# One branch instead of two in the last expert pair, whole combination ahead of its up projection, and an output norm that passes through PSUM

## The chip, the cores and the metric

The kernel runs on one core of one Trainium2 chip. The metric is the device time of one execution in microseconds (us), median of the runs shown. All times of the trace are counted from the start of the profiled execution's span.

## The reference

Two layers over 512 tokens of width 1024 (float32). Each layer is a mixer and a mixture of experts, each with a residual and a layer norm behind it. Layer 0's mixer has two convolutions, layer 1's a spatial gating unit and chunked attention.

```
for layer in range(2):
    mix = conv_shortconv_mixer(x, ...) if layer % 2 == 0 else sgu_chunk_attention_mixer(x, ...)
    x = layer_norm(ALPHA * x + mix, mix_ln_g[layer], mix_ln_b[layer])
    ffn = hierarchical_moe(x, ...)      # 4 groups x 8 experts, the two best of one group
    x = layer_norm(ALPHA * x + ffn, ffn_ln_g[layer], ffn_ln_b[layer])
...
hb = silu(xb @ w_gate[e]) * (xb @ w_up[e]);   y = hb @ w_down[e]
```

An expert's gate and up matrices are 1024 x 512, its down matrix 512 x 1024. All 32 experts of a layer are run, whatever the routing.

## The kernel before, in words

**The experts.** `experts()` runs the 32 experts of a layer as 16 pairs, g = 0 to 15. A pair has 128 slots, 64 for each expert. Tokens that do not fit into them are treated in conditional code. For each pair TensorE (PE) does, in this order:

- the gate projection into PSUM tile `pg` (32 matmuls, L746); ScalarE (ACT) turns it into `sg` (L756)
- the up projection into `pu` (32 matmuls, L746); VectorE (DVE) multiplies `sg` and `pu` to the hidden tile `h` (L761)
- four transposes of `h` (L767), which ACT copies to `hT` (L769)
- a branch, `If v > 0` (L1156), on a count `v` that the routing left in `nxi`: behind it lies `overflow(v)`, code for slots that are full. It is skipped here in nearly all pairs
- the down projection in two halves, `py` (16 matmuls each, L746). ACT and DVE split each half into a high and a low part `y` (L779, L780).

**The combination.** `combine(S, *prev, ts)` adds the output of the pair before to the accumulator `acc`: for each of 4 token tiles and 2 halves a pair of matmuls with the one-hot matrix `S` (L790, L791) and one DVE addition (L799). In the last pair two of the four tiles are combined ahead of the up projection and two behind it (L1127, L1141).

**The general loop.** `crowded()` (L1035) holds a general loop over all pairs for inputs with very many tokens on an expert. It stands ahead of the last pair's gate, in an `If most > 0` (L1037). Here it is skipped in both layers, so each engine jumps over its body. `most` is counted, and PE gets a hint of the branch, at the end of pair 14. PE alone gets hints, in the other branches too. Behind it `last()` loads the first weights of the next mixer (L1609).

**The end of a layer.** The last pair's output is combined half by half by `Last.half` (L801 ff.): PE puts `acc` of tiles 0 and 1 into PSUM (L815), adds the spread of `y`, and DVE takes the statistics (L826). Tiles 2 and 3 are added on DVE (L825). `hat()` (L284) normalises tiles 0 and 1 on ACT, out of PSUM into `acc`, tile by tile. Layer 0 goes on in `mixer1` with `turn(0)`, transposes of `acc` (L1341), then matmuls against high and low parts of the weights (L1377 ff.). Layer 1 goes on in `output()`, which scales by `gf` and adds `bf`: GpSimd (POOL) on 3.5 of the 4 halves of tiles 0 and 1 (L1592, L1593), DVE on the rest. Of tiles 2 and 3, DVE does the norm itself, two operations per half (L1602, L1603). Each finished half is written to the output.

**Order of the work.** Each engine executes its own instructions in the order of the program. A branch is executed by every engine. The weights come over the queue of SyncE (SP), in the order of `ws.load`.

Of the kernel before, what the change touches and what calls it, by code (L numbers as in the profile page):

```python
# [31 lines left out]
PQ = 256  # L32
# [11 lines left out]
def trunk(ctx: ExitStack, tc: tile.TileContext, a, out, layers=2, moe=True):  # L44
# [236 lines left out]
    def hat(t, mr, ys):  # L281
        n = D // len(ys)
        for h, y in enumerate(ys):
            ACT.activation(acc[:, t, h * n:(h + 1) * n], y, AF.Identity, bias=mr[2], scale=mr[1])  # L284
# [157 lines left out]
    class Router:  # L442
# [178 lines left out]
        def counts(self):  # L621
# [8 lines left out]
            nxs = small([2 * NP + 1], "nxs")  # L630
# [13 lines left out]
            DVE.tensor_reduce(nxs[:, 2 * NP:], m, axis=AX.X, op=OP.max)  # L644
            nxi = small([2 * NP + 1], "nxi", I32)
# [118 lines left out]
    def hidden_T(h):  # L764
        p = mtile((128, 4, 128))
        for j in range(4):
            PE.transpose(p[:, j], h[:, j * 128:(j + 1) * 128], ident)  # L767
        hT = wk.tile([128, 4, 128], F32, name="hT", tag="q2")
        ACT.activation(hT, p, AF.Copy)  # L769
        return hT  # L770
# [30 lines left out]
    class Last:  # L801
# [6 lines left out]
        def half(self, h, S, yh, yl):  # L808
# [9 lines left out]
            for t in range(NT):  # L818
                if t == 2 and h:
                    self.mrs = self.finish(0)  # L820
                    self.lead(1)
                    for i in range(2):
                        hat(i, self.mrs[i], self.ys[i])
# [146 lines left out]
    def count(nxi, i, **kw):  # L970
        return nc.values_load(nxi[0:1, i:i + 1], min_val=0, max_val=NTHR + 1,
# [6 lines left out]
    def experts(rt, ws, T1, pt, x1d, xt, xg, xg2, update, last, last2, lead, finish):  # L978
# [56 lines left out]
        def crowded():  # L1035
            slots = ws.order[6:8]
            with tc.If(most > 0, label=f"most{ws.l}", preferred_fallthrough_block=True):  # L1037
                for g in range(NP):
                    v, cond = when(nxi, NP + g, 0)
                    with cond:  # L1040
# [4 lines left out]
                        with tc.For_i(0, v, 1):  # L1045
# [9 lines left out]
                            h3 = hidden_T(hidden(h3, proj2("u", xo, *u)))  # L1055
                            u = [ws.fetch(0, 4 + j, slots[j], g) for j in range(2)]
                            y3 = down(h3, *u, T3.wt[:, 0:1], (yh, yl))
                            combine(onehot_S(T3.tk[:, 0:1], "q2"), *y3)

        for g in range(NP):  # L1060
            W = lambda j: ws.u[6 * g + j]
            own, own2 = EVEN if COLS[g] < HEAVY else ODD
            if g == NP - 1:
                crowded()
                last()
# [58 lines left out]
            if g:  # L1124
                S = onehot_S(col(T1.tk, g - 1))
                if g == NP - 1:
                    combine(S, *prev, (0, 1))  # L1127
# [5 lines left out]
            if g > 1:  # L1133
                v = count(nxi, COLS[g])
# [5 lines left out]
            else:  # L1140
                combine(S, *prev, range(2 if g == NP - 1 else 0, CM if g < NP - 1 else NT))  # L1141
# [13 lines left out]
            if g > 1:  # L1155
                with tc.If(v > 0, label=skip, preferred_fallthrough_block=True):  # L1156
                    overflow(v)
# [5 lines left out]
            if g == NP - 2:  # L1163
                most = count(nxi, 2 * NP)
                tc.mark_branch_hint_location(f"most{ws.l}", most > 0, engines=[ET.PE])
# [162 lines left out]
    def mixer1(prev, ws):  # L1328
# [32 lines left out]
        ys, mrs = combine_last(prev, lambda: turn(0))  # L1361
# [221 lines left out]
    def output(prev):  # L1583
# [11 lines left out]
        for t, s in ((0, slice(0, 512)), (0, slice(512, 1024)), (1, slice(0, 512)), (1, slice(512, 512 + PQ))):  # L1595
            scale_shift(POOL, t, s)
        scale_shift(DVE, 1, slice(512 + PQ, 1024))
        for t in (2, 3):
            for h in range(2):
                s = slice(512 * h, 512 * h + 512)  # L1600
                x = acc[:, t, s]
# [108 lines left out]
```

## Time and profile before

| | us |
|---|---|
| median of 3 runs (1438.19 to 1445.37) | 1443.88 |
| profiled execution, its own time | 1442.83 |
| its span | 1440.9 |
| PE busy | 1333.4 (93%) |
| DVE busy | 684.5 (48%) |
| ACT busy | 370.3 (26%) |
| POOL busy | 294.7 (20%) |
| mean granted clock of PE | 0.976 |

The profiled execution is 1.05 us under the median. A share of busy time is a mean over stages. The last pair of either layer and the stretch behind it are short, and there the waits count: what one engine was waiting for, and when that came.

### The profile page before, as it was taken

How to read it: one execution, taken by the hardware profiler on the slowest of the kernel's cores; microseconds unless marked ns; L12 is line 12 of the kernel's file. 1: busy time of each engine (PE TensorE's matmuls, PEld its weight loads, DVE VectorE, ACT ScalarE, POOL GpSimd, SP SyncE). 2: the span in 40 equal slices, each digit the busy share in tenths (PEclk: the TensorE clock that was granted, in tenths of full speed). 3: DMA queues.
4: the chain of work that ended last, by engine and by line, in shares of the span. 5: the costliest groups of instructions: out<-in, count | busy, mean ns of one | idle time of the engine just before them, and what ended most of it. 6: DMA issues, size and time to landing. Idle time of an engine off the chain costs nothing. (4 is left out here: it accounts for less than half of the span.)

```text
span 1440.9 us, 19633 instructions
## 1 busy us (share of the span) xinstructions
PE 1333.4 (93%) x7322; PEld 705.9 (49%) x7322; DVE 684.5 (48%) x1412; ACT 370.3 (26%) x701; POOL 294.7 (20%) x262
## 2 busy tenths in 40 slices
PE   9989999998999998898899999999999999989984
PEld 6777764333353334333586767834333444333331
DVE  7997688323342223322628554794322343322326
ACT  5545541111111111111525555511111111111101
POOL 5784620000000000000653239200000000000002
PEclk9999999999999999999999999999999999999997
DMA  7505469999999999999500037689999999999971
GB/s 294 234 5 212 175 243 428 419 424 422 419 403 412 422 419 426 422 418 354 206 1 1 23 133 315 257 338 421 420 425 424 421 394 420 427 422 422 423 301 59
DMA packets 56837, 461.21 MB, mean 320 GB/s; under 512 B 8804, under 2 KB 9444, under 8 KB 33232
## 3 DMA queue, kind: packets, MB, share of 16 engines
q1 hardware_dynamic: 51184, 449.96, 75.8%
q0 software_dynamic: 4608, 7.79, 1.5%
q8 instruction: 102, 1.67, 0.5%
q10 hardware_dynamic: 864, 1.13, 0.2%
q14 instruction: 79, 0.65, 0.1%
HBM read 461.56 MB, written 6.29 MB: 325 GB/s over the span
## 5 line engine op out<-in xcount | busy, mean ns | idle before, releaser
L746 PE MATMUL py<-w,hT 128*64 128x512 f32 (+1 forms) x1280 | 243.2, 617 | 22.3 <-issue 11.6
L746 PE MATMUL pu<-w,xt 128*64 128x512 f32 (+1 forms) x1280 | 244.2, 607 | 19.8 <-DMA w<-in_w_up_dram 19.8
L746 PE MATMUL pg<-w,xt 128*64 128x512 f32 (+1 forms) x1280 | 233.4, 599 | 10.9 <-ACTq L1037 10.9
L761 DVE TENSOR_TENSOR h<-sg,pu 128x512 f32<-128x512 f32 x32 | 22.0, 688 | 355.9 <-issue 302.1
L691 POOL DMA_INDIRECT xg<-x1d,idx x30 | 29.7, 990 | 780.2 <-PE m L439 677.9
L746 PEld LDWEIGHTS pu<-w,xt 128*64 128x64 f32 (+1 forms) x1280 | 78.3, 129 | 176.3 <-issue 143.2
L799 DVE TENSOR_TENSOR acc<-acc,m 128x512 f32<-128x512 f32 x240 | 148.6, 680 | 19.3 <-PE m L791 17.3
L746 PEld LDWEIGHTS pg<-w,xt 128*64 128x64 f32 (+1 forms) x1280 | 76.2, 128 | 163.1 <-issue 140.8
L746 PEld LDWEIGHTS py<-w,hT 128*64 128x64 f32 (+1 forms) x1280 | 72.4, 128 | 154.5 <-issue 150.4
L780 DVE SCALAR_TENSOR_TENSOR y<-py,wt,y 128x512 fp32r<-128x512 f32 x64 | 48.0, 750 | 199.2 <-ACT y L779 199.2
L779 ACT ACTIVATE y<-py,wt 128x512 fp32r<-128x512 f32 x64 | 44.0, 687 | 302.9 <-PE py L746 302.9
L790 PE MATMUL m<-y,S 128*128 128x512 f32 x248 | 106.1, 428 | 0.0
L791 PE MATMUL m<-y,S 128*128 128x512 f32 x248 | 98.0, 395 | 0.0
L109 POOL TENSOR_TENSOR wl<-win,wh 128x512 fp32r<-128x512 f32 x64 | 84.2, 1331 | 65.6 <-ACT wh L108 65.4
L769 ACT ACTIVATE hT<-m 128x512 f32<-128x512 f32 x32 | 19.1, 597 | 292.4 <-PE m L767 270.5
L109 POOL TENSOR_TENSOR wl<-wo,wh 128x512 fp32r<-128x512 f32 x64 | 82.1, 1309 | 38.2 <-ACT wh L108 37.8
L756 ACT ACTIVATE sg<-pg 128x512 f32<-128x512 f32 x32 | 19.1, 597 | 217.3 <-PE pg L746 217.3
L790 PEld LDWEIGHTS m<-y,S 128*128 128x128 f32 x248 | 46.8, 189 | 39.3 <-issue 26.9
L128 PE MATMUL m<-xh,wl 128*128 128x512 f32 x144 | 57.6, 400 | 3.0 <-POOL wl L109 3.0
L127 PE MATMUL m<-xh,wh 128*128 128x512 f32 x144 | 57.4, 399 | 0.8 <-ACT wh L108 0.8
L129 PE MATMUL m<-xl,wh 128*128 128x512 f32 x144 | 56.8, 394 | 0.0
L791 PEld LDWEIGHTS m<-y,S 128*128 128x128 f32 x248 | 46.9, 189 | 7.9 <-DVE y L780 1.0
(446 smaller groups left out, 1881.2 us busy)
## 6 DMA issues: line engine op xcount, KB each, us to landing
w<-in_w_gate_dram SPq DMA_DIRECT2D x64, 2048.0 KB, 24.9
w<-in_w_up_dram SPq DMA_DIRECT2D x50, 2048.0 KB, 18.2
w<-in_w_down_dram SPq DMA_DIRECT2D x50, 2048.0 KB, 21.0
w<-in_w_up_dram SPq DMA_DIRECT2D x40, 512.0 KB, 25.0
w<-in_w_down_dram SPq DMA_DIRECT2D x40, 512.0 KB, 22.8
win<-in_w_in_dram SPq DMA_DIRECT2D x18, 512.0 KB, 7.8
wo<-in_w_out_dram SPq DMA_DIRECT2D x4, 2048.0 KB, 12.3
w<-in_w_up_dram SPq DMA_DIRECT2D x8, 1024.0 KB, 15.8
```

The source lines that it names most:

```text
L109: POOL.tensor_tensor(l, src, h, op=OP.subtract)
L127: PE.matmul(p, wh[:, j], xh[:, k], start=(k == 0), stop=False)
L128: PE.matmul(p, wl[:, j], xh[:, k], start=False, stop=False)
L129: PE.matmul(p, wh[:, j], xl[:, k], start=False, stop=(k == KD - 1))
L691: POOL.indirect_dma_start(out=dst, out_offset=None, in_=x1d, in_offset=bass.IndirectOffsetOnAxis(ap=idx_col, axis=0), bounds_check=T - 1, ...
L746: PE.matmul(p[w * c:w * c + w], x[:, w * c:w * c + w], ww[own[w * c // SUB]], **kw)
L761: DVE.tensor_mul(h, sg, pu)
L779: ACT.activation(yh[:, s], p, AF.Copy, scale=wt)
L780: DVE.scalar_tensor_tensor(yl[:, s], p, wt, yh[:, s], op0=OP.mult, op1=OP.subtract)
L790: PE.matmul(p, S[:, t * 128:(t + 1) * 128], yh[:, s], start=start, stop=False)
L791: PE.matmul(p, S[:, t * 128:(t + 1) * 128], yl[:, s], start=False, stop=True)
L799: DVE.tensor_add(acc[:, t, s], acc[:, t, s], p)
```

## The change

It has five parts.

1. **One branch.** The counts `nxi` get one more entry, the sum of `most` and the last pair's count. The branch on `most` ahead of the last pair is gone. The last pair's branch (L1156) asks for the sum. Inside it stand a branch to the pair's overflow code and, behind that, the branch to the general loop. `last()` follows behind. The hint to PE stands ahead of the up projection, as in other pairs.
2. **Combination.** In the last pair all four tiles are combined ahead of the up projection, none between it and the transposes.
3. **Norm of tiles 0 and 1** half by half: tile 0 and 1 first halves, then tile 0 and 1 second halves.
4. **Ten filler matmuls** (`keep_warm(10)`, bf16, 128 x 512) ahead of `turn(0)`.
5. **Output norm.** ACT writes the normed halves of tiles 2 and 3 into PSUM (`pg`, `pu`, `py`, `py`); DVE multiplies there by `gf`, and adds `bf` into `acc`. POOL does all four halves of tiles 0 and 1.

```
-            DVE.tensor_reduce(nxs[:, 2 * NP:], m, axis=AX.X, op=OP.max)
-            nxi = small([2 * NP + 1], "nxi", I32)
+            DVE.tensor_reduce(nxs[:, 2 * NP:2 * NP + 1], m, axis=AX.X, op=OP.max)
+            TT(nxs[:, 2 * NP + 1:], nxs[:, 2 * NP:2 * NP + 1], n[:, COLS[-1]:COLS[-1] + 1], op=OP.add)
+            nxi = small([2 * NP + 2], "nxi", I32)
...
-                    for i in range(2):
-                        hat(i, self.mrs[i], self.ys[i])
+                    for j in range(2):
+                        for i in range(2):
+                            hat(i, self.mrs[i], self.ys[i], j)
...
-            with tc.If(most > 0, label=f"most{ws.l}", preferred_fallthrough_block=True):
+            with when(nxi, 2 * NP, 0)[1]:
...
-            if g == NP - 1:
-                crowded()
-                last()
...
-                    combine(S, *prev, (0, 1))
+                    combine(S, *prev)
...
-                v = count(nxi, COLS[g])
+                v = count(nxi, COLS[g] if g < NP - 1 else 2 * NP + 1)
...
-                combine(S, *prev, range(2 if g == NP - 1 else 0, CM if g < NP - 1 else NT))
+                combine(S, *prev, range(0, CM if g < NP - 1 else 0))
...
                 with tc.If(v > 0, label=skip, preferred_fallthrough_block=True):
-                    overflow(v)
+                    if g < NP - 1:
+                        overflow(v)
+                    else:
+                        v1, cond = when(nxi, COLS[g], 0)
+                        with cond:
+                            overflow(v1)
+                        crowded()
+                if g == NP - 1:
+                    last()
...
-            if g == NP - 2:
-                most = count(nxi, 2 * NP)
-                tc.mark_branch_hint_location(f"most{ws.l}", most > 0, engines=[ET.PE])
...
-        ys, mrs = combine_last(prev, lambda: turn(0))
+        def first_turn():
+            keep_warm(10)
+            turn(0)
+        ys, mrs = combine_last(prev, first_turn)
...
-        for t, s in ((0, slice(0, 512)), (0, slice(512, 1024)), (1, slice(0, 512)), (1, slice(512, 512 + PQ))):
-            scale_shift(POOL, t, s)
-        scale_shift(DVE, 1, slice(512 + PQ, 1024))
+        norms = {}
+        for t in (2, 3):
+            for h in range(2):
+                p = norms[t, h] = ptile("gu"[h] if t == 2 else f"y{h}")
+                ACT.activation(p, ys[t][h], AF.Identity, bias=mrs[t][2], scale=mrs[t][1])
+        for t in (0, 1):
+            for h in range(2):
+                scale_shift(POOL, t, slice(512 * h, 512 * h + 512))
...
-                x = acc[:, t, s]
-                DVE.scalar_tensor_tensor(x, ys[t][h], mrs[t][0], gf[:, s], op0=OP.subtract, op1=OP.mult)
-                DVE.scalar_tensor_tensor(x, x, mrs[t][1], bf[:, s], op0=OP.mult, op1=OP.add)
+                p = norms[t, h]
+                TT(p, p, gf[:, s], op=OP.mult)
+                TT(acc[:, t, s], p, bf[:, s], op=OP.add)
```

The order of the instructions on ACT, around the end of layer 0's pair 14 and the last pair. Line numbers of the changed kernel are a few higher: L779 is L781 there, L756 is L758, L769 is L771. In the kernel before:

```order
L779 ACTIVATE y<-py_10645,wt_1956 128x512
L703 ACTIVATE xt<-m,gb 128x128 x4
L779 ACTIVATE y<-py_10675,wt_1956 128x512
L1037 COMPARE_AND_BRANCH
...
L1037 UNCONDITIONAL_BRANCH
L756 ACTIVATE sg<-pg 128x512
L971 TENSOR_LOAD nxi
L769 ACTIVATE hT<-m 128x512
L1156 COMPARE_AND_BRANCH
```

In the changed kernel:

```order
L781 ACTIVATE y<-py_10666,wt_1957 128x512
L758 ACTIVATE sg<-pg 128x512
L974 TENSOR_LOAD nxi
L771 ACTIVATE hT<-m 128x512
L1156 COMPARE_AND_BRANCH
L974 TENSOR_LOAD nxi
L1161 COMPARE_AND_BRANCH
...
L1156 UNCONDITIONAL_BRANCH
L806 ACT_TABLE_LOAD
L806 ACTIVATE warm<-mean_w 128x1
L781 ACTIVATE y<-py_14301,wt_1957 128x512
```

The long body (225 listed rows of ACT between branch and target in the kernel before, 252 in the changed one) has moved from ahead of `sg` to behind `hT`, and the jump over the short body is gone.

PE at the same place, in the kernel before:

```order
L746 MATMUL py_10675<-w,hT 64x512 x8
L1037 COMPARE_AND_BRANCH
...
L1037 UNCONDITIONAL_BRANCH
L746 MATMUL pg<-w,xt 64x512 x16
L790 MATMUL m<-y,S 128x512
L791 MATMUL m<-y,S 128x512
...
L746 MATMUL pu<-w,xt 64x512 x16
...
L767 MATMUL m<-ident,h 128x128 x4
L1156 COMPARE_AND_BRANCH
```

In the changed kernel:

```order
L748 MATMUL py_10666<-w,hT 64x512 x8
L748 MATMUL pg<-w,xt 64x512 x16
L792 MATMUL m<-y,S 128x512
L793 MATMUL m<-y,S 128x512
...
L1135 REGISTER_ALU
L1719 BRANCH_PREFETCH_HINT
L748 MATMUL pu<-w,xt 64x512 x16
L769 MATMUL m<-ident,h 128x128 x4
L1156 COMPARE_AND_BRANCH
```

The 16 combining matmuls (L792, L793) now stand together between the gate and up projections, nothing stands between the up projection and the transposes, and one branch is left.

DVE at the end of the program, in the kernel before:

```order
L275 SCALAR_TENSOR_TENSOR mvr<-mv_29012,mvr 128x2
L1592 TENSOR_TENSOR acc<-acc,gf 128x256
L1593 TENSOR_TENSOR acc<-acc,bf 128x256
L1602 SCALAR_TENSOR_TENSOR acc<-acc,mv_29012,gf 128x512
L1603 SCALAR_TENSOR_TENSOR acc<-acc,mvr,bf 128x512
```

In the changed kernel:

```order
L274 SCALAR_TENSOR_TENSOR mvr<-mv_29035,mvr 128x2
L1615 TENSOR_TENSOR pg<-pg,gf 128x512
L1616 TENSOR_TENSOR acc<-pg,bf 128x512
L1615 TENSOR_TENSOR pu<-pu,gf 128x512
L1616 TENSOR_TENSOR acc<-pu,bf 128x512
```

The two operations on 128 x 256 are gone from DVE. Four pairs of operations remain, now with one operand in PSUM each (two of the four are shown on the changed side, one on the other).

## Rows read from the trace of the kernel before

**Rows 1.** What PE waited for, whole program: us in total, times, longest.

```profile
PE pg L746 <- ACTq L1037: 10.9, 2, 5.5
```

**Rows 2.** Timeline of PE, last pair of layer 0: start, us, instruction, idle before.

```profile
655.17 8.46 PE L746 MATMUL pg<-w,xt 128*64 128x512 f32 x32 [5.45 <-ACTq L1037]
...
674.60 0.60 PE L767 MATMUL m<-ident,h 128*128 128x128 f32 x4
675.94 3.65 PE L746 MATMUL py<-w,hT 128*64 128x512 f32 x16 [0.74 <-ACTq L1156]
```

**Rows 3.** Timeline of PE, last pair of layer 1.

```profile
1384.82 8.86 PE L746 MATMUL pg<-w,xt 128*64 128x512 f32 x32 [5.44 <-ACTq L1037]
...
1405.98 3.65 PE L746 MATMUL py<-w,hT 128*64 128x512 f32 x16 [0.74 <-ACTq L1156]
```

**Rows 4.** Windows: us, busy (x) PE, PEld, DVE, ACT, POOL; PEclk, DMA share, GB/s.

```profile
655.17:663.56 8.39, 8.39 (x33) 2.55 (x33) 0.48 (x1) 0.00 (x0) 0.00 (x0) 0.83 0.87 314
665.62:672.64 7.02, 7.02 (x33) 2.21 (x33) 1.19 (x2) 0.00 (x0) 0.00 (x0) 1.00 1.01 430
...
1384.82:1393.61 8.79, 8.79 (x33) 2.62 (x33) 0.49 (x1) 0.00 (x0) 0.00 (x0) 0.79 0.91 338
1395.66:1402.67 7.01, 7.01 (x33) 2.21 (x32) 1.19 (x2) 0.00 (x0) 0.00 (x0) 1.00 0.44 167
```

**Rows 5.** Line 1037 (the long jump), 640 to 700 us: ns, first and last start.

```profile
L1037 ACTq EVENT_SEMAPHORE  x2: 17/17/17, 655.1 to 655.2; - x2
...
L1037 ACTq COMPARE_BRANCH  x1: 45/45/45, 649.8 to 649.8; - x1
```

**Rows 6.** Line 1037, whole program, PE's own sequencer, one jump in each layer.

```profile
L1037 PEldq COMPARE_BRANCH  x2: 2867/4458/6049, 646.1 to 1375.7; - x2
```

**Rows 7.** Line 1156 (the short jump), 640 to 700 us.

```profile
L1156 ACTq COMPARE_BRANCH  x1: 45/45/45, 675.3 to 675.3; - x1
L1156 ACTq EVENT_SEMAPHORE  x1: 17/17/17, 675.9 to 675.9; - x1
```

**Rows 8.** Timeline of DVE, last pair of layer 0, the hidden tile.

```profile
672.83 0.69 DVE L761 TENSOR_TENSOR h<-sg,pu 128x512 f32<-128x512 f32 x1 [6.02 <-PE pu L746]
```

**Rows 9.** Timeline of ACT, last pair of layer 0, the copy `hT`.

```profile
675.29 0.60 ACT L769 ACTIVATE hT<-m 128x512 f32<-128x512 f32 x1 [10.96 <-PEq L1156]
```

**Rows 10.** DMA queues of the page: packets, MB, share of 16 engines.

```profile
q14 instruction: 79, 0.65, 0.1%
```

**Rows 11.** Timeline of ACT behind layer 0, the four normed halves.

```profile
693.15 2.79 ACT L284 ACTIVATE acc<-m,mvr 128x512 f32<-128x512 f32 x4 [0.87 <-DVE mvr L275]
```

**Rows 12.** Timeline of PE behind layer 0, the transposes.

```profile
693.98 0.33 PE L1341 MATMUL m<-ident,acc 128*128 128x128 f32 x1 [3.25 <-ACT acc L284]
695.32 3.31 PE L1341 MATMUL m<-ident,acc 128*128 128x128 f32 x15 [1.01 <-ACT acc L284]
```

**Rows 13.** Timeline of PE, filler matmuls at the start and later.

```profile
0.93 4.45 PE L148 MATMUL m<-onesb 128*128 128x512 bf16 x10 [0.93 <-DVE onesb L163]
...
198.17 1.25 PE L148 MATMUL m<-onesb 128*128 128x512 bf16 x5
```

**Rows 14.** Timeline of DVE at the program's end.

```profile
1423.51 0.67 DVE L825 TENSOR_TENSOR acc<-acc,py 128x512 f32<-128x512 f32 x1
...
1427.43 0.91 DVE L275 SCALAR_TENSOR_TENSOR mvr<-mv,mvr 128x2 f32<-128x2 f32 x1
...
1430.00 1.75 DVE L1602 SCALAR_TENSOR_TENSOR acc<-acc,mv,gf 128x512 f32<-128x512 f32 x1
...
1436.94 0.75 DVE L1603 SCALAR_TENSOR_TENSOR acc<-acc,mvr,bf 128x512 f32<-128x512 f32 x1
```

**Rows 15.** Timeline of POOL at the program's end, its first operation.

```profile
1423.16 1.26 POOL L1592 TENSOR_TENSOR acc<-acc,gf 128x512 f32<-128x512 f32 x1 [78.99 <-ACT acc L284]
```

**Rows 16.** Groups by shape: ACT from SBUF into PSUM.

```profile
L312 ACT ACTIVATE py<-apad,par 128x512 f32<-128x512 f32 x2 | 1.6, 782 | 7.2 <-DVE apad L398 7.2
```

**Rows 17.** DMA issues of the page or its view: KB each, us to landing.

```profile
out_dram<-acc SPq DMA_DIRECT2D x4, 256.0 KB, 2.0
```

More of the change, by code (lines that the diff above doesn't have):

```diff
@@ L31 @@
 CM = 1
-PQ = 256
 W0 = 10
@@ L279, in two, with hat @@
         return [y[:, 0:512], y[:, 512:1024]]
-    def hat(t, mr, ys):
+    def hat(t, mr, ys, only=None):
         n = D // len(ys)
         for h, y in enumerate(ys):
+            if only not in (None, h):
+                continue
             ACT.activation(acc[:, t, h * n:(h + 1) * n], y, AF.Identity, bias=mr[2], scale=mr[1])
@@ L629, in counts @@
                 TT(over[:, i], cs, lim[:, i], op=OP.is_gt)
-            nxs = small([2 * NP + 1], "nxs")
+            nxs = small([2 * NP + 2], "nxs")
             n, m = nxs[:, 0:NP], nxs[:, NP:2 * NP]
@@ L762, in hidden, with hidden_T @@
         return h
-    def hidden_T(h):
+    def hidden_T(h, tag="q2"):
         p = mtile((128, 4, 128))
@@ L767, in hidden_T @@
             PE.transpose(p[:, j], h[:, j * 128:(j + 1) * 128], ident)
-        hT = wk.tile([128, 4, 128], F32, name="hT", tag="q2")
+        hT = wk.tile([128, 4, 128], F32, name="hT", tag=tag)
         ACT.activation(hT, p, AF.Copy)
@@ L970, in count @@
     def count(nxi, i, **kw):
-        return nc.values_load(nxi[0:1, i:i + 1], min_val=0, max_val=NTHR + 1,
+        return nc.values_load(nxi[0:1, i:i + 1], min_val=0, max_val=NTHR + 1 + WIDE,
                               skip_runtime_bounds_check_because="a count of blocks", **kw)
@@ L1054, in crowded @@
                             u = [ws.fetch(0, 2 + j, slots[j], g) for j in range(2)]
-                            h3 = hidden_T(hidden(h3, proj2("u", xo, *u)))
+                            h3 = hidden_T(hidden(h3, proj2("u", xo, *u)), "q3")
                             u = [ws.fetch(0, 4 + j, slots[j], g) for j in range(2)]
                             y3 = down(h3, *u, T3.wt[:, 0:1], (yh, yl))
-                            combine(onehot_S(T3.tk[:, 0:1], "q2"), *y3)
+                            combine(onehot_S(T3.tk[:, 0:1], "r"), *y3)
         for g in range(NP):
```

## The prediction

> **What bounds the kernel now.** I read the page first (PE is busy for 93% of the span), then the list of what PE waited for, then the timelines around the largest wait that the diff touches. That wait is the long jump: PE stands twice for some 5.5 us ahead of the last pair's gate, for ACT's sequencer at line 1037 [rows 1]. The timelines show it in both layers [rows 2, 3]: the end of pair 14's down projection lies at 655.17 - 5.45 = 649.72 and at 1384.82 - 5.44 = 1379.38 us. The wait for ACT is a jump, not work: ACT took its branch at 649.8 and sent its event at 655.1, so the long jump takes 5.3 us [rows 5]. The short jump over a pair's overflow code takes 675.9 - 675.3 = 0.6 us [rows 7]. In the last pair itself PE waits for no weights, so it is paced by PE's own work and by these jumps. Behind the long wait PE's granted clock is low: the gate takes 8.39 us at 0.83, where the same 32 matmuls of up take 7.02 at 1.00; in layer 1 it is 8.79 at 0.79 against 7.01 [rows 4]. [...] At the program's end DVE and POOL share the output norm and DVE ends last: its last operation ends at 1437.69, and its half lands 2.0 us later [rows 14, 17].
>
> **1. The branch moves.** The order of instructions shows that the long body now lies between ACT's `hT` and the down projection. I therefore take the long jump as kept and moved: 5.3 us there, in place of the 0.6 of the short one.
>
> Before, from the end of pair 14 to the last pair's `py`: 675.94 - 649.72 = 26.22 us in layer 0, 1405.98 - 1379.38 = 26.60 in layer 1 [rows 2, 3].
>
> After, step by step, at the full clock:
> - gate 7.02, up 7.02 [rows 4]
> - the combination, moved together between them, is the same 16 matmuls: 665.62 - 663.56 = 2.06 and 674.60 - 672.64 = 1.96, so 4.02 [rows 2, 4]
> - then nothing covers the chain of the hidden tile any more. DVE's product starts 672.83 - 672.64 = 0.19 behind up and takes 0.69 [rows 8]; ACT starts `hT` 675.29 - 674.60 = 0.69 behind the first transpose [rows 2, 9]. Together 1.57, with handing over 1.6. Before, combining matmuls hid most of DVE's product
> - ACT reaches its branch as it starts `hT` (675.3 for both, [rows 7, 9]). From there the jump's 5.3 us, and 0.1 to PE's start.
>
> That makes 18.06 + 1.6 + 5.4 = 25.0 us: 1.2 less in layer 0, 1.6 less in layer 1. The clock is then low for the down projection in place of the gate. I price it as before, +1.4 and +1.8. So with an unchanged jump both layers come to +0.2 us.
>
> The jump in layer 1 may be shorter. It was measured while the weights were flowing (DMA share 0.87 to 1.01 around it); in layer 1 it now begins near 1379.4 + 18.1 + 1.6 = 1399 us, where the weights run out (share 0.44 from 1395.66 to 1402.67) [rows 4]. No row shows this jump beside idle DMA. I bound it by 5.3 above and by the 2.87 us of PE's shorter long jump below [rows 6], and take 4.1, midway: layer 1 then gives -1.0 us (bounds -4.0, with no cost of the clock, to +0.2). Layer 0 stays at +0.2 (-1.2, no cost of the clock, to +0.2).
>
> What waits behind: PE's `py` waits for ACT, with nothing queued ahead of it. DVE's jump starts when it has issued the product, about 1.4 us ahead of ACT's. PE's own jump took 2.87 and 6.05 us [rows 6]; it starts as the transposes are issued, about 0.5 to 0.9 behind up, and so ends at the latest with ACT's (1.6 + 5.4 = 7.0 behind up). The extra DVE addition in the routing is one tiny operation per layer, the count and hint of pair 14 go: nothing, since the counts are needed some pairs later. The loads of `last()` stood behind the long jump before and stand behind it now: nothing, while SP lands as before.
>
> **2. Norm half by half and ten fillers, layer 0 only.** ACT's four halves take 2.79 us from 693.15, so the first is done at 693.9 [rows 11]. Before, PE transposed at the low clock: 15 in 3.31 us, until 698.63 [rows 12]. Ten fillers take 2.5 us at the full clock (5 in 1.25) and 4.45 at the low one [rows 13]. [...] The fillers come behind 3.25 us of idling [rows 12], so some of them run at the low clock, and what follows them does not: I take +0.6.
>
> **3. Output norm.** DVE's last small operation ends at 1427.43 + 0.91 = 1428.34. ACT then writes a half into PSUM in 0.78 us [rows 16], so DVE starts near 1429.1. It now has eight plain operations with one PSUM operand each. The nearest row is an addition with one PSUM operand, 0.67 us while POOL was working [rows 14, 15]. Eight take 5.4: end 1434.5, landing 1436.5 against 1439.7: -3.2 us. POOL has eight of 1.26 from 1423.16, until 1433.2 and, landed, 1435.2: just not the end [rows 15]. Bounds: nothing gained, if DVE's operations are slowed beside POOL as the 1.75 us of its first old one was [rows 14]; -4.5, if POOL is what ends last.
>
> **Sum** for the profiled execution: +0.2 - 1.0 + 0.6 - 3.2 = -3.4 us, 1442.83 - 3.4 = **1439.4 us**. It stands 1.05 us under the median of 1443.88; against that the forecast is 4.5 us or 0.3%. The time of faster by 0.5% would be 1436.7, of slower 1451.1; 0.5% (7.2 us) is about what a measurement here can tell, the three runs themselves lying 7.2 us apart.
>
> **The rivals.**
>
> *The long jump goes away (0.13).* If the merged branch lands as fast as the short one, `py` starts 675.94 - 675.29 = 0.65 behind `hT`'s start [rows 2, 9]: 18.06 + 1.6 + 0.65 = 20.3 us, 5.9 and 6.3 less, and PE stays at the full clock. With the other terms (+0.6, -3.2): 1428.0 us. [...] Against it: ACT jumped over 225 rows before and took 5.3 us for it [rows 5], in layer 1 PE waited just as long (5.44), and what is fetched comes in pieces of 0.65 MB / 79 = 8.2 KB [rows 10].
>
> [...]
>
> *PE lands last (0.06), the slower side.* PE's long jump would be served behind the hint's own fetch, or only when `py` is released. Its price is one more jump of PE in either layer, 2.87 to 6.05 us [rows 6]: -3.4 + 5.7 to 12.1, so 1445 to 1451.5 us. It decides if PE's event at the merged branch comes later than ACT's. Against it: PE's jump had a hint before as well, and ended before ACT's.
>
> *The tail gains nothing (0.09).* DVE's operations beside POOL stay at 1.2 to 1.8 us as the old ones did; the rest stands: 1442.6 us. For it: one operand of each still lies in SBUF. Against it: the addition of 0.67 had SBUF operands too [rows 14].
>
> **How the numbers follow.** The forecast's case has 0.72. Its own bounds add up to -1.2 - 4.0 - 0.4 - 4.5 = -10.1 and +0.2 + 0.2 + 3.3 + 0 = +3.7, so 1432.7 to 1446.5; this also holds the third rival and half of the second. What lies outside is the first rival (0.13) and the rest of the second (0.03), and some 0.04 for the spread of runs: 2 in 10. Faster by over 0.5%: 0.13, and 0.11 of the forecast's own case (a short jump in layer 1 together with the tail's gain): 0.24. Slower by over 0.5%: 0.04. Within: 0.72.
>
> **What would show it.** Right: PE's list of waits has no line for a branch ahead of the last gate, but about 5.3 us (layer 0) and 4 us (layer 1) ahead of the last pair's first `py`, put down to ACT's branch; a gate of 7.0 us at clock 1.00; a first `py` half of 5 us instead of 3.65; DVE's eight last operations near 0.67 us each, the last ending near 1434.5. Wrong: a wait under 1 us there (the first rival), an event of PE later than ACT's (the second), DVE operations over 1 us at the end (the third), or fillers over 4 us with `turn(0)` ending behind 700.

## The result, and the profile after

The changed kernel took 1430.95 us (median of 5 runs, 1429.7 to 1435.42) against 1443.88 for the kernel before: a ratio of 0.9921, with a 95% interval of 0.9898 to 0.9944. Two more comparisons gave 0.9899 (0.9875 to 0.9922) and 0.9925 (0.9898 to 0.9951). So it gains 11 to 15 us, where the prediction said 3.4 to 4.5. The first profiled execution took 1432.51 us, against 1442.83.

What PE waited for in the changed kernel, whole program (us in total, times, longest):

```profile
PE pu L748 <- DMA w<-in_w_up_dram: 21.4, 10, 3.6
PE py L748 <- issue: 11.9, 4, 3.7
PE py L748 <- DVEq L1156: 5.4, 2, 3.3
...
PE py L748 <- PEq L1156: 2.9, 1, 2.9
```

The 10.9 us ahead of the gate [rows 1] are gone, as predicted, and a wait ahead of the last pair's `py` has come. It is 5.4 us, not 9.3, and it is put down to DVE's sequencer, not to ACT's. The timeline of PE for the last pair of layer 0, and below it the same place in layer 1:

```profile
648.58 7.04 PE L748 MATMUL pg<-w,xt 128*64 128x512 f32 x32
...
667.47 0.66 PE L769 MATMUL m<-ident,h 128*128 128x128 f32 x4 [0.86 <-DVE h L763]
670.16 5.35 PE L748 MATMUL py<-w,hT 128*64 128x512 f32 x16 [2.04 <-DVEq L1156]
675.45 1.98 PE L817 MATMUL m<-acc,ident 128*128 128x512 f32 x4
...
1372.70 7.51 PE L748 MATMUL pg<-w,xt 128*64 128x512 f32 x32
...
1396.05 6.28 PE L748 MATMUL py<-w,hT 128*64 128x512 f32 x16 [3.33 <-DVEq L1156]
1402.26 1.12 PE L817 MATMUL m<-acc,ident 128*128 128x512 f32 x2
```

Layer 0's gate takes 7.04 us, at a granted clock of 1.00 (648.58 to 655.60 us), where it took 8.46 [rows 2]; layer 1's takes 7.51, at 1.00 too. The gate now follows pair 14 without a gap, so the stretch from the end of pair 14 to `py` is 670.16 - 648.58 = 21.6 us (26.2 before, 25.0 predicted), in layer 1 23.4 (26.6 before, 23.8 predicted: 25.0 with the shorter jump). The first half of `py` then pays for the standstill: 5.35 and 6.28 us, at a granted clock of 0.68 and 0.57, in place of 3.65 [rows 2] at 1.00.

Line 1156 in the changed kernel, 640 to 700 us (ns; first and last start): the merged branch of layer 0.

```profile
L1156 DVEq EVENT_SEMAPHORE  x2: 21/21/21, 669.9 to 670.0; - x2
L1156 ACTq EVENT_SEMAPHORE  x2: 17/17/17, 670.7 to 670.8; - x2
...
L1156 DVEq COMPARE_BRANCH  x1: 56/56/56, 666.8 to 666.8; - x1
L1156 PEldq COMPARE_BRANCH  x1: 428/428/428, 667.5 to 667.5; - x1
L1156 ACTq COMPARE_BRANCH  x1: 45/45/45, 668.2 to 668.2; - x1
```

Two things are to be seen. ACT's jump took 670.7 - 668.2 = 2.5 us, not 5.3 [rows 5]; DVE's took 3.1. And `py` started at 670.16, ahead of ACT's event and behind DVE's: PE waits for DVE here, whose jump begins as the hidden product starts, 1.4 us before ACT's. In layer 1 ACT's jump took 3.3 us and DVE's 4.3. Windows show the DMA around it (columns as in [rows 4]), first the changed kernel ahead of the branch and during DVE's jump in layer 0, then the same in layer 1:

```profile
660.00:666.80 6.80, 6.60 (x32) 2.01 (x28) 1.26 (x3) 0.00 (x0) 0.00 (x0) 1.00 0.07 27
666.80:669.90 3.10, 0.66 (x4) 0.42 (x4) 0.61 (x1) 0.60 (x1) 0.00 (x0) 1.00 0.44 85
1385.00:1391.30 6.30, 6.20 (x30) 1.87 (x26) 0.78 (x2) 0.00 (x0) 0.00 (x0) 1.00 0.82 305
1391.30:1395.80 4.50, 0.66 (x4) 0.42 (x4) 0.69 (x1) 0.60 (x1) 0.00 (x0) 0.86 0.12 42
```

and the kernel before, ahead of the jump of layer 0 and during it:

```profile
645.00:649.80 4.80, 4.71 (x25) 1.92 (x24) 2.03 (x5) 2.10 (x6) 0.00 (x0) 1.00 1.01 413
649.80:655.10 5.30, 0.00 (x0) 0.00 (x0) 0.75 (x1) 0.68 (x1) 0.00 (x0) 0.95 0.96 365
```

The last two numbers of a row are the DMA share and GB/s. Before, the jump fell into full queues; now it falls where they are nearly empty or running empty (27 GB/s ahead of it in layer 0, 42 during it in layer 1), since the pair's weights have landed and the next loads come behind the branch. Those next loads are the first of `last()`. SP issued them at 662.74 us before, and they filled the queues at the place to which the jump has moved (share 1.01 from 665.62 to 672.64, [rows 4]). Now SP issues them only when PE is past the merged branch (its event came at 668.2), while DVE's and ACT's jumps are under way. SP's timeline before, then in the changed kernel:

```profile
662.74 1.54 SPq L1609 DMA_DIRECT2D wval<-in_w_in1t_dram  x2
```

```profile
668.24 2.08 SPq L1622 DMA_DIRECT2D wval<-in_w_in1t_dram  x2
```

The tail came as predicted. DVE's end, then POOL's, in the changed kernel:

```profile
1420.12 0.91 DVE L274 SCALAR_TENSOR_TENSOR mvr<-mv,mvr 128x2 f32<-128x2 f32 x1
1421.95 0.70 DVE L1615 TENSOR_TENSOR pg<-pg,gf 128x512 f32<-128x512 f32 x1 [0.91 <-ACT pg L1607]
1422.68 0.69 DVE L1616 TENSOR_TENSOR acc<-pg,bf 128x512 f32<-128x512 f32 x1
...
1426.68 0.69 DVE L1616 TENSOR_TENSOR acc<-py,bf 128x512 f32<-128x512 f32 x1
```

```profile
1415.86 1.26 POOL L1600 TENSOR_TENSOR acc<-acc,gf 128x512 f32<-128x512 f32 x1 [73.74 <-ACT acc L285]
...
1424.88 1.26 POOL L1601 TENSOR_TENSOR acc<-acc,bf 128x512 f32<-128x512 f32 x1
```

From POOL's first operation to DVE's end it takes 1427.37 - 1415.86 = 11.5 us, 14.5 before [rows 14, 15]. DVE's operations with one PSUM operand take 0.69 to 0.70 us beside POOL.

### The profile page after: what moved, and what is told of

It is laid out like the page before. It is cut to its first block, busy times and chain, and to the rows that moved or that the text cites. A ratio compares the mean times of both kernels' runs of the same rounds, so it can differ in the third digit from the quotient of the medians.

```text
span 1430.7 us, 19616 instructions
## 1 busy us (share of the span) xinstructions
PE 1332.0 (93%) x7332; PEld 699.8 (49%) x7332; DVE 681.4 (48%) x1412; ACT 373.5 (26%) x705; POOL 294.7 (21%) x262
## 5 line engine op out<-in xcount | busy, mean ns | idle before, releaser
L748 PE MATMUL py<-w,hT 128*64 128x512 f32 (+1 forms) x1280 | 247.6, 624 | 25.3 <-issue 11.9
L748 PE MATMUL pg<-w,xt 128*64 128x512 f32 (+1 forms) x1280 | 229.5, 594 | 0.4 <-DMA w<-in_w_gate_dram 0.4
L781 ACT ACTIVATE y<-py,wt 128x512 fp32r<-128x512 f32 x64 | 44.0, 687 | 305.1 <-PE py L748 305.1
L792 PE MATMUL m<-y,S 128*128 128x512 f32 x248 | 106.0, 427 | 0.0
L793 PE MATMUL m<-y,S 128*128 128x512 f32 x248 | 97.9, 395 | 0.0
L771 ACT ACTIVATE hT<-m 128x512 f32<-128x512 f32 x32 | 19.1, 597 | 294.8 <-PE m L769 294.8
L758 ACT ACTIVATE sg<-pg 128x512 f32<-128x512 f32 x32 | 19.1, 597 | 202.6 <-PE pg L748 202.6
L792 PEld LDWEIGHTS m<-y,S 128*128 128x128 f32 x248 | 46.7, 188 | 38.3 <-issue 25.3
L107 ACT ACTIVATE wh<-win 128x512 fp32r<-128x512 f32 x64 | 38.9, 625 | 46.1 <-PE pg L128 13.6
```

The costliest lines, as they stand in the source:

```text
L107: ACT.activation(h, src, AF.Copy)
L748: PE.matmul(p[w * c:w * c + w], x[:, w * c:w * c + w], ww[own[w * c // SUB]], **kw)
L781: ACT.activation(yh[:, s], p, AF.Copy, scale=wt)
L792: PE.matmul(p, S[:, t * 128:(t + 1) * 128], yh[:, s], start=start, stop=False)
L793: PE.matmul(p, S[:, t * 128:(t + 1) * 128], yl[:, s], start=False, stop=True)
```

## The experiments

Each ratio is to the kernel before on the same chip, with its 95% interval. Two theories stood at the start. **Queue**: the code behind a long jump is fetched by DMA and has to wait while weights are loaded, so the jump is short where their queues are empty. **Code**: it is short because of where branch and target now lie.

### Loads put back beside the jump

```
+                if g == NP - 1:
+                    for s in ws.order[6:8]:
+                        nc.sync.dma_start(unit(s, [128, KD, 512], F32, "wval"), a["w_in1t"][0])
                 with tc.If(v > 0, label=skip, preferred_fallthrough_block=True):
```

> The changed kernel, with two loads of 2 MB each (read by nobody) put on SP's queue ahead of the merged branch in both layers, into ring slots that are free there. Queue theory: the merged jump was shorter than the 5.3 us of the old one because its instruction fetch found the DMA queues nearly empty (DMA share 0.07 and 0.82 ahead of it, 0.01 and 0.20 at it, against 0.96 to 1.02 before). Then with the loads flowing ACT's jump goes from 2.54 and 3.30 us back to 5.0 to 5.5 in both layers, DVE's from 3.14 and 4.33 to 5.3 to 5.7, PE's wait ahead of the last pair's py from 2.04 and 3.33 to 4 to 5 us, and the time from 1431 to 1434 to 1438. Code theory (the jump is shorter by where its branch and target now lie in the code): both jumps stay within 0.5 us of 2.54 and 3.30 (ACT), and the time stays within 2 us of the changed kernel's.

Ratio 0.9967 (0.9944 to 0.9991), median 1437.14 us. Line 1159 is the merged branch of this kernel; layer 0, then layer 1:

```profile
L1159 ACTq EVENT_SEMAPHORE  x2: 17/17/17, 672.4 to 672.5; - x2
L1159 DVEq EVENT_SEMAPHORE  x2: 21/21/21, 674.2 to 674.3; - x2
...
L1159 DVEq COMPARE_BRANCH  x1: 56/56/56, 668.3 to 668.3; - x1
...
L1159 ACTq COMPARE_BRANCH  x1: 45/45/45, 669.7 to 669.7; - x1
```

```profile
L1159 DVEq EVENT_SEMAPHORE  x2: 21/21/21, 1405.9 to 1406.0; - x2
L1159 ACTq EVENT_SEMAPHORE  x2: 17/17/17, 1406.9 to 1407.0; - x2
...
L1159 DVEq COMPARE_BRANCH  x1: 56/56/56, 1400.0 to 1400.0; - x1
...
L1159 ACTq COMPARE_BRANCH  x1: 45/45/45, 1401.5 to 1401.5; - x1
```

DVE's jump is back at 5.9 us in both layers, ACT's at 5.4 in layer 1; PE waits 4.8 us ahead of `py` in both. That is the queue theory; only ACT's jump in layer 0 stayed at 2.7. The stretch from the end of pair 14 to `py` is 24.3 and 24.7 us.

The DMA records of the traces show the fetch itself, one packet of 8.2 KB on queue q14 behind each of these branches in layer 0 (which packet is whose is read from their times). In the changed kernel DVE branches at 666.75 and a packet starts at 668.04, 1.3 us later; in the kernel before it is 3.5 us. Here ACT's packet starts 0.9 us behind its branch, as in the changed kernel, and DVE's 3.9, which is why ACT's jump stayed short. The transfer takes 0.3 to 0.5 us in all of these, and the event comes 1.1 to 1.6 us behind its end. So it is the wait for the packet's start that loads lengthen. With the general loop left out (the next run) no such packet comes there in layer 0.

The load just ahead of DVE's branch orders its jumps in the profiled executions: with a DMA share of 0.0 to 0.1 in the 2 us ahead (layer 0 of the ten kernels and repeats with the merged branch and no loads put back) they take 2.8 to 3.4 us; with 0.3 to 0.6 (layer 1 of the same) 3.8 to 4.3; with 0.8 to 1.1 (the kernel before, and this run) 5.5 to 5.9. The 2 us ahead in the changed kernel, layers 0 and 1 (columns as in [rows 4]):

```profile
664.75:666.75 2.00, 1.85 (x10) 0.40 (x6) 0.03 (x1) 0.00 (x0) 0.00 (x0) 1.00 0.00 0
1389.35:1391.35 2.00, 1.85 (x10) 0.39 (x6) 0.03 (x1) 0.00 (x0) 0.00 (x0) 1.00 0.58 217
```

The price of the long jump is 2.5 to 4.3 us for ACT and DVE where the queues had run empty or were running empty, 5.1 to 5.9 with full ones, but for the 2.7 of ACT above.

### The general loop left out

```
                         with cond:
                             overflow(v1)
-                        crowded()
```

> The changed kernel without the general loop for crowded inputs (it leaves that code out; the branch then jumps over the pair's overflow code alone). This prices what is left of the long jump. All theories: ACT's jump about 0.6 us and DVE's about 1.3, PE's wait ahead of py 0.7 us or less in both layers, both halves of py at 3.65 us with no loss by the clock. Sum against the profiled run of the changed kernel: -1.4 and -2.6 for the jumps, -1.7 and -2.6 for the clock: about 8 us less, 1423. If the cold clock is due to something else than that standstill, only 4 us less.

The profiled execution took 1427.88 us, with the jump as expected in layer 0: `py` 20.2 us behind pair 14, both halves at 3.65. But the median of 11 runs was 1437.34, a ratio of 0.9971 (0.9957 to 0.9984): slower than the changed kernel. What PE waited for in the profiled execution:

```profile
PE py L748 <- issue: 16.5, 7, 3.5
...
PE py L748 <- PEq L1156: 8.8, 3, 3.2
```

PE's waits ahead of `py` that are put down to its own sequencer or to nothing shown (issue) are 25.3 us here, 14.8 in the changed kernel; one of them, 3.16 us, stands at the branch of layer 1's last pair. Leaving the loop out moves all code behind it; that this made PE's short jumps slower was not tried by itself. Nor do these waits explain the median, since the execution that has them was the fastest of the 11 and had the highest mean granted clock, 0.982; the ten others had 0.970 to 0.979. So this run does not price the jump by its median; its profile does for layer 0: 1.4 us, and the clock.

### Hints for ACT and DVE

```
-                tc.mark_branch_hint_location(skip, v > 0, engines=[ET.PE])
+                tc.mark_branch_hint_location(skip, v > 0, engines=[ET.PE] if g < NP - 1 else [ET.PE, ET.Activation, ET.DVE])
```

> The changed kernel with the hint of the last pair's branch given to ACT and DVE as well as to PE. Queue theory: the hint starts the fetch 7 us or more ahead of the branch, so that ACT's and DVE's jumps take about 0.6 and 1.3 us and the result is that of the kernel without the general loop, some 8 us under the changed kernel. Rival: the hint does nothing for these engines, or the fetched block is given up again before the branch: jumps and time stay (within 2 us).

Ratio 0.9929 (0.9901 to 0.9958), median 1430.43: the rival. ACT's jumps took 2.6 and 3.1 us, DVE's 2.9 and 4.0, at most 0.3 less than without. The hint did next to nothing for these two engines. The DMA records show no packet that these hints brought: from the gate's start to DVE's branch two packets start on q14 in either layer, as without them, and behind the branches two more, as without them.

### Fillers at the standstill

```
             hT = hidden_T(h)
+            if g == NP - 1:
+                keep_warm(8)
```

> The changed kernel with 8 filler matmuls (bf16, 128 x 512) on PE behind the last pair's transposes, ahead of the branch, in both layers. If the slow first half of py (5.35 and 6.28 us in place of 3.65) is due to the standstill at the jump, the fillers (2.0 us at the full clock) fit into the waits of 2.04 and 3.33 us, the halves come back to 3.7 to 4.5 us and the time falls by 2 to 4 us, to 1427 to 1429. If the fillers come too late to hold the clock, the halves stay above 5 us and the time within 1 us of the changed kernel, or later by the part of the fillers that does not fit.

PE in the last pair of layer 0, then of layer 1:

```profile
670.17 1.91 PE L147 MATMUL m<-onesb 128*128 128x512 bf16 x8
672.64 3.65 PE L748 MATMUL py<-w,hT 128*64 128x512 f32 x16 [0.56 <-PEq L1158]
...
1399.88 1.91 PE L147 MATMUL m<-onesb 128*128 128x512 bf16 x8
1402.94 3.65 PE L748 MATMUL py<-w,hT 128*64 128x512 f32 x16 [1.15 <-DVEq L1158]
```

The halves are back at 3.65 us in both layers: the slow `py` was the low clock behind the standstill (0.68 and 0.57 in the first profile of the changed kernel). Layer 1 shows it best: in eight executions with the merged branch and without fillers the half took 5.2 to 6.6 us there. In layer 0 it took 3.65 without fillers too, in two of the eight. The stretches to the first ident matmul (L817) take 25.4 and 26.6 us, against 26.9 and 29.6 in the first profile of the changed kernel. Yet the median was 1434.31, ratio 0.9933 (0.9912 to 0.9954): no gain that can be told.

### The first part undone, twice

```
+            if g == NP - 1:
+                crowded()
+                last()
...
-                v = count(nxi, COLS[g] if g < NP - 1 else 2 * NP + 1)
+                v = count(nxi, COLS[g])
...
+            if g == NP - 2:
+                most = count(nxi, 2 * NP)
+                tc.mark_branch_hint_location(f"most{ws.l}", most > 0, engines=[ET.PE])
```

> The changed kernel with its first part undone: the branch to the general loop stands ahead of the last pair's gate again, with its own count and hint, and the pair's own short branch behind hT; all other parts are as in the changed kernel. Queue theory: the weights flow at that place, so ACT's jump is 5.3 and DVE's 5.5 us again, PE waits 5.4 ahead of the gate and 0.7 ahead of py, the gate takes 8.4 to 8.9 us. The stretch from the end of pair 14 to the first ident matmul behind py grows from 26.9 and 29.6 us back to 29.5 to 30.5 in both layers: 3 to 4 us in all, 1434 to 1436. Rival: the change's gain comes from these stretches to more than 6 us, 1437 or more; or from none of them, under 1433.

Median 1447.43 of 12 runs, ratio 1.0019 (1.0000 to 1.0039). In the profile the place is as expected:

```profile
PE pg L748 <- ACTq L1040: 10.6, 2, 5.4
```

with stretches of 30.7 and 30.5 us. So the rival's number (1437 or more) came, but not its reason: these stretches are 4.8 us longer than the changed kernel's first ones (26.9, 29.6), and the median 16 us.

> The kernel of the run with the first part undone, once more, for a second profile: its first profile was of its fastest execution (1440.0 of 1440.0 to 1453.5 us). Chance theory: the two stretches of the last pairs (end of pair 14 to the first ident matmul) take 30.7 and 30.5 us again within 0.7, and what this execution is slower by (up to 7 us) lies in stretches that the change does not touch, as time at the low clock and as one slowed DVE operation in the second routing (0.97 or 3.54 us so far). Rival: the last pairs' stretches are longer by 2 us or more in the usual execution.

It took 1441.11 us, with stretches of 32.1 and 30.7. Both profiled executions lie below all other runs of this kernel (1443.1 to 1453.5). So what those lose is in neither profile. The runs' record shows what goes with it: the two profiled executions had a mean granted clock of 0.978, the eleven others 0.971 to 0.977, and the slowest five of them 0.971 or 0.972. Where the clock was lost stays open.

### The tail alone, and the tail taken out

The fifth part put on the kernel before:

> The kernel before with the output norm of the changed one alone (fifth part). From POOL's first scaling operation to the end of DVE's last one it takes 11.5 us in place of 14.5: 3 us under the kernel before, 1439.5 where that has 1442.6. Rival: the tail gains only together with the norm half by half, which lets POOL start the second tile earlier: less than 1.5 us.

Median 1438.97, ratio 0.9967 (0.9948 to 0.9986), and 11.5 us from POOL's first operation to DVE's end: the 3 us, with the norm still tile by tile. The other way round, the changed kernel with the old output norm:

> The changed kernel without the fifth part (the output norm as in the kernel before). From POOL's first operation to DVE's last 14.5 us in place of 11.5: 3 us above the changed kernel. Rival: more than 5 us, if the parts help each other.

Median 1437.97, ratio 0.9940 (0.9917 to 0.9962), the tail 14.5 us again. Both ratios allow 3 us.

### Each kernel once more

> The kernel before once more, with a profile of its own: how far two executions of one program differ, and where. Chance theory: outside the stretches that the change touches (end of the last pairs, boundary, tail) the profiled runs of the two kernels differ by 3.8 us, and two profiled runs of this one program differ by as much, at places like the wait for the sums of the routing (1.6 to 4.0 us so far) and the first convolution. Rival: the two executions agree within 1 us, so that the 3.8 us belong to the change (moved code).

It took 1442.55 us. At pair 0 of layer 0 it was 3.2 us ahead of the first profile, at pair 15 it was level. In the last pair of layer 0 its gate took 9.98 us, so that the stretch is 31.4 us, not 29.8.

> The changed kernel once more: its ratio to the kernel before on another chip job, and a second profile. Chance theory: the ratio stays between 0.990 and 0.996, ACT's and DVE's jumps within 0.5 us of 2.54/3.30 and 3.14/4.33, while the unchanged stretches differ by some us from the first profile. Rival: unchanged stretches agree within 1 us with the first profile of the same kernel.

Median 1431.46, ratio 0.9899; but the profiled execution took 1438.51, 6 us more than the first one. The difference is at other places: the fillers ahead of the mixer take 4.01 us (2.35 in the first profile, at a granted clock of 1.00), and one DVE operation of layer 1's routing takes 3.54 instead of 0.97 us, with POOL at work beside it in both. The second profile, then the first:

```profile
875.82 3.54 DVE L473 TENSOR_TENSOR rwg<-rw,gb 128x288 f32<-128x288 f32 x1 [1.84 <-DMA gb<-in_lncol_dram]
```

```profile
874.15 0.97 DVE L473 TENSOR_TENSOR rwg<-rw,gb 128x288 f32<-128x288 f32 x1 [1.91 <-DMA gb<-in_lncol_dram]
```

PE waits 4.0 instead of 1.6 us for it. So profiled executions of one program differ by up to 6 us for reasons of this kind, and the last pairs have to be compared by themselves.

### Moved, not merged

```
                 with tc.If(v > 0, label=skip, preferred_fallthrough_block=True):
                     overflow(v)
                 if g == NP - 1:
                     crowded()
                     last()
```

> The changed kernel with its two branches apart: the pair's own short one behind hT, then the one to the general loop (with its own hint to PE), then the first loads of the next mixer. So the long jump is moved but not merged. Queue theory: the long jump is as short as merged (ACT 2.5 to 3.3, DVE 3.1 to 4.3 us), and comes one short jump of DVE (1.1 to 1.3 us) later: PE's wait ahead of py 3.0 to 3.5 us in layer 0 and 4.3 to 4.8 in layer 1, 2 to 3 us in all over the changed kernel. Rival: merging is what made it short; apart, the long jump takes 5 us or more again.

Median 1445.97, ratio 1.0001 (0.9981 to 1.0021). ACT's long jump stayed short (2.8 us), and still PE waited 7.0 us in layer 0 and 3.9 in layer 1. PE's sequencer at the two branches, layer 0:

```profile
L1159 PEldq COMPARE_BRANCH  x1: 3899/3899/3899, 668.0 to 668.0; - x1
```

```profile
L1040 PEldq COMPARE_BRANCH  x1: 2937/2937/2937, 672.1 to 672.1; - x1
```

In the merged kernel PE's branch takes 0.4 us. With two hints ahead of up, neither of PE's two jumps was quick in layer 0, and the second took 3.0 us in layer 1 too. The DMA records fit this. With one hint a packet starts on the instruction queue q8 (PE's, by the times) 1.0 to 3.9 us behind it, ahead of the branch, and PE's branch takes 0.3 to 0.5 us; so it is in both layers of all eleven executions with the merged branch over the long body. Here, in layer 0, no packet comes between the two hints (659.37 and 659.96) and the first branch, and in layer 1 one comes for the two. Without the general loop none came in layer 1 either, and there PE's branch took 3.3 us. So merging matters after all, not for ACT and DVE but for PE; two branches with one hint were not tried. In layer 0 this is the sign of the prediction's second rival, PE's event behind ACT's (675.1 and 672.2), but not its reason, a jump served behind the hint's own fetch. The stretches to the first ident matmul are 33.6 and 29.3 us (26.9 and 29.6), 6.4 us more together; the median lies further above the changed kernel's than that, and the rest was not traced to a place; its ten runs have a mean granted clock of 0.973 on average, as the kernel before has.

### The second and the fourth part undone

> The changed kernel with its second part undone: two of the four token tiles are combined behind the up projection again. DVE then has four additions (2.5 us) between its hidden product and the branch, so its jump starts about 2 us later behind up and PE's py with it, while 2 us of combining lie under it: the stretch from the end of pair 14 to py stays within 1.0 us of 21.6 and 23.4 us, PE waits 2 us more ahead of py in each layer. Rival: DVE's sequencer runs ahead of its additions, so that its jump starts as early as now: the stretch is 1.5 to 2 us shorter in each layer and the second part costs time.

```
-                    combine(S, *prev)
+                    combine(S, *prev, (0, 1))
...
-                combine(S, *prev, range(0, CM if g < NP - 1 else 0))
+                combine(S, *prev, range(2 if g == NP - 1 else 0, CM if g < NP - 1 else NT))
```

Stretches to `py` of 21.9 and 23.0 us (21.6 and 23.4), waits of 3.3 and 3.9; ratio 0.9924 (0.9896 to 0.9951). The second part is worth nothing either way: PE works through 2 us of combining that it otherwise idles.

> The changed kernel without the ten filler matmuls ahead of the first transposes of layer 1's mixer (part four undone, the norm half by half kept). From the last combining matmul of layer 0 to the mixer's first matmul it took 7.9 us before and 8.1 now. If the fillers are worth nothing there, it takes 7.5 to 8.3 without them, with the transposes at the low clock (3.3 us); if they hold the clock for the stretch behind, the mixer's first 3.7 us show a granted clock under 0.95 without them and the time rises by 0.5 to 1.5 us. Rival: they cost: without them the stretch is shorter by over 0.5 us.

Median 1430.05 of 4, ratio 0.9884 (0.9858 to 0.9911). From the second group of ident matmuls to the mixer's first matmul it is 10.8 us, against 11.5, 13.2 and 11.5 in three profiles of the changed kernel and 11.4 before: the fillers cost 0.7 us or more. They did hold the clock (granted clock of the mixer's first 3.7 us: 1.00 with them, 0.79 without), but it does not pay: the eighth of the mixer's groups of three matmuls starts 16.5 us behind the second ident group without them, 16.7, 18.4 and 16.7 with them. Without them the transposes start at the first normed half, since the halves come in the order in which they are wanted:

```profile
690.91 0.33 PE L1346 MATMUL m<-ident,acc 128*128 128x128 f32 x1 [3.25 <-ACT acc L285]
691.58 1.09 PE L1346 MATMUL m<-ident,acc 128*128 128x128 f32 x8 [0.34 <-ACT acc L285]
692.91 1.75 PE L1346 MATMUL m<-ident,acc 128*128 128x128 f32 x7 [0.25 <-ACT acc L285]
```

### The first part alone

> The kernel before with the first part alone: one merged branch behind hT, two of four tiles combined behind up as before, norms and tail as before, no fillers. Queue theory: ACT's and DVE's jumps take 2.5 to 3.3 and 3.1 to 4.3 us, the stretches from the end of pair 14 to the first ident matmul behind py are 25.5 to 27.5 and 28 to 30 us in place of 30.9 and 30.1, 5 to 7 us in all: a ratio to the kernel before of 0.995 to 0.9965. Rival (the run with this part undone): it carries 10 us or more, a ratio under 0.993.

Median 1434.71, ratio 0.9923 (0.9893 to 0.9952). PE waits 3.1 and 3.8 us ahead of `py`, for DVE's sequencer in both:

```profile
PE py L747 <- DVEq L1154: 6.8, 2, 3.8
```

The stretches are 27.0 and 28.8 us, so the profile shows 3.6 and 1.3 us less than in the two profiles of before (30.6 and 30.1 on average). The ratio says 7 to 15 us. This part carries most of the gain, and the timed runs give it more than the profile does.

### A version from these

Fillers at the jump, none at the boundary, beside the changed kernel on the same chip:

> The changed kernel with 8 fillers between the last pair's transposes and the branch, in both layers, and without the 10 ahead of layer 1's first transposes. Both halves of py at 3.65 us in both layers as with the fillers alone (25.4 and 26.6 us for the stretches in place of 25.9 and 28.5 on average), and 0.5 to 1.5 us less at the boundary: 2 to 4 us under the changed kernel on the same chip, if the fillers' gain does not come back as low clock at another place. Rival: within 2 us of the changed kernel.

> The changed kernel itself, on the same chip as the three others, to compare them with. Its ratio to the kernel before again between 0.988 and 0.994.

Median 1430.17, ratio 0.9901 (0.9877 to 0.9924), with stretches of 25.4 and 26.9 us and a boundary of 10.8. The changed kernel itself: median 1434.94, ratio 0.9925 (0.9898 to 0.9951). The version is under both kernels by its median, clearly so under the kernel before; of the changed kernel its interval does not part it.

## Why the prediction was wrong

The measured time, 1430.95 us, lies under the range (1432.7 to 1446.5) and near the first rival (1428.0, given 0.13).

- **The long jump taken as kept at 5.3 us.** This is the step that failed. The text itself gave the reason: it allowed a shorter jump in layer 1, since the weights run out there, and took it as unchanged in layer 0. But in layer 0 the loads that kept the queues full before were those of `last()`, and the change moved them behind the branch; the prediction put that move down as worth nothing. With loads put back, the stretch to `py` is 24.3 and 24.7 us; without, 21.6 and 23.4. So empty queues are worth 2.7 us in layer 0 and 1.4 in layer 1. In the sum it is layer 0's term: +0.2 was put for it, and by the stretch to the first ident matmul it measured -2.9 in the two first profiles, -4.4 on average. With that the forecast for a profiled execution would have been 1436.3 to 1434.8, inside the range; what took the timed runs under it besides is told below. For layer 1 the estimate of the stretch (23.8) was right, in part by luck: from ACT's branch to `py` it took 3.3 us where 4.2 was taken, and the gate 7.4 where 7.0 was.
- **PE waiting for ACT.** It waits for DVE, whose jump is longer but begins 1.4 us earlier. The prediction saw the earlier start and gave DVE's jump no length; in the trace of before it took 656.0 - 650.5 = 5.5 us. That is the difference between 25.0 and the 24.3 to 24.7 us with full queues.
- **The clock** was seen rightly: the gate came back to 7.04 us in layer 0, and `py` paid, by 1.7 and 2.6 us in the first profile (1.4 and 1.8 were priced, the gate less up in [rows 4]), by 0 and 1.7 in the second, by 1.7 in both layers in the third.
- **The boundary**: +0.6 was said. From the second ident group to the mixer's first matmul, three profiles of the changed kernel average 12.1 us, two of before 11.5: +0.6. No run shows the bounds of -0.4 and +3.3 that stand for it in the range, and +0.6 was a choice between them; the three profiles, 11.5, 13.2 and 11.5, lie 0.0 to 1.7 above 11.5. In the first of them ten fillers took 2.35 us and 16 transposes 1.91, both at a granted clock of 1.00, where before 15 transposes took 3.31 [rows 12] at 0.53. The view of the 4.45 us [rows 13] has a clock of 1.00, so no low clock is shown there.
- **The tail**: -3.2 was said, -3.0 came, with DVE at 0.69 us where 0.67 was taken.
- **The first rival** came near in size, not by its mechanism: the jump did not become as short as the short one. The second did not happen in the changed kernel, as PE's branch took 0.4 us. The third fell.

Put together from the profiles: the last pairs gain 4.4 and 1.3 us (averages of three profiles after, 26.2 and 28.8, against two before, 30.6 and 30.1), the tail 3.0, and the boundary gives back 0.6: 8.1 us. The profiled executions differ by 6.3 on average (1442.83 and 1442.55 against 1432.51, 1438.51 and 1438.05). The timed runs gain 11 to 15 us, 3 to 7 more. None of the stretches that were compared shows these, but the record of the runs shows what goes with them, the mean granted clock of each execution. It was 0.9731 on average in the 67 runs of the kernel before that have it and 0.9765 in 17 of the changed kernel. Within either kernel a run is 0.9 to 1.0 us shorter for every 0.001 of clock. The averages differ by 10.9 us. By an estimate from all 84 runs, with one slope for both kernels, 7.8 of them (6.6 to 9.0) are left at equal clock, which is near what the profiles add up to, and the other 3.1 go with 0.0034 more clock. The profiled executions of before (0.976 twice) had more clock than its average run, those of the changed kernel (0.979, 0.972 and 0.973) on average less than its own, so that they lie only 6.3 us apart. Why the changed kernel's runs have more of the full clock, and at which places, was not shown: a mean clock goes with the time and need not be its cause. Even executions of one program differ at single places, as the repeated profiles show: ten fillers 2.35 or 4.01 us, one DVE operation beside POOL 0.97 or 3.54.

## What to carry to other kernels

A skipped branch over a long body had a price here, and the price depended on what the DMA queues carried when it was taken (DVE 2.8 to 4.3 us with them empty or running empty, 5.5 to 5.9 with them full): put it where the weights have landed, and the next loads behind it. Before pricing a wait for a branch, see which engine's event the waiting instruction needs and when that engine reaches the branch. If several engines must jump, one branch with one hint for PE was worth more here than two with hints 0.6 and 0.8 us apart (PE's branch 0.4 us, against 3.9 and 2.9 in layer 0). And before a small gain is put down to a change, compare the granted clock of the runs: here, by estimate, 0.0034 of it went with 3.1 of 10.9 us.

## What the runs showed of the hardware that was not expected

- The same long jump took DVE 2.8 to 4.3 us with the DMA queues empty or running empty and 5.5 to 5.9 with them full; ACT 2.5 to 3.3 and, but for one jump of 2.7, 5.1 to 5.4. What grew was the wait for the instruction packet to start, from 1.3 to 3.5 us and more, and not its transfer, 0.3 to 0.5.
- With one hint, and its packet ahead of the branch, PE's branch in the last pair took 0.3 to 0.5 us (3.3 in the one case where no packet came); given to ACT and DVE as well, the hint saved them at most 0.3 us.
- Two hints given to PE 0.6 us apart: in layer 0 no instruction packet for PE ahead of the branches, and jumps of 3.9 and 2.9 us.
- Eight filler matmuls of 1.9 us in all, put into a standstill of 2 to 3 us, brought the next 16 matmuls from 5.2 to 6.6 us (layer 1, eight executions without fillers) to 3.65.
- With code left out at one place, PE's waits ahead of `py` that are put down to its own sequencer or to nothing shown were 25.3 us, where three profiles of the changed kernel have 14.8, 11.8 and 12.1.
